# Two groups of products side by side at each phase start, and eight operand groups turned by blocks

## The chip, the cores and the metric

The kernel runs on one core of one Trainium2 chip. Its time is the device time of one execution in microseconds (us). Before the change the median of three runs is 2881.62 us (2881.26 to 2881.76).

## The reference

Two transformer blocks of width 2048 are applied in turn to 256 tokens, in float32. What costs time is the products with the weights, each of which is read once:

```python
# first block
proj = rms_norm(x) @ w_in             # q, k, v, gla q/k/v/r, decay gate, conv, 3 merge gates
mixed = g0 * (attn @ w_br_attn) + g1 * (gla @ w_br_gla) + g2 * (conv @ w_br_conv)
x = x + mixed @ w_out
h2 = rms_norm(x)
x = x + (silu(h2 @ w_ffn_gate) * (h2 @ w_ffn_up)) @ w_ffn_down
x = rms_norm(x)
# second block
proj = rms_norm(x) @ w_in_2 + b_in_2  # q, k, v, u of a scan, 2 gates
merged = sig(ga) * (attn2 @ w_branch_attn) + sig(gs) * (ssm @ w_branch_ssm)
x = x + merged @ w_out_2
val, gate = split(rms_norm(x) @ w_up)
x = x + (val * gelu(conv(gate))) @ w_down
return rms_norm(x)
```

The widths: 15376 columns in w_in, 5632 in the feed-forward, 5888 in w_in_2. Attention, gated linear attention and the scan work on 256 tokens and are small beside the weights.

## The kernel before

**Products.** A weight matrix is cut into groups of up to 512 columns (`prod` appends a Group). A group's k runs over tiles of 128 rows, 16 of them for width 2048. For the accuracy of float32 each operand is split into a high and a low part, and a product is three matmuls (lines 1395 to 1397): high by high, high by low, low by high, for each of the two halves of the tokens. A *unit* is four k-tiles, 1 MB of weights in one DMA (line 1358), with three buffers in turn; a *step* is two k-tiles, twelve matmuls. ACT writes the high part of the weights (line 165) and VectorE the low part (line 166), three steps ahead, into four buffers. The program has 1012 steps, numbered from 0.

**Operands.** The left side of a product is the activations, with the features on the partitions. So what one group of columns gives, 256 tokens by 512 features, must be transposed and split before it can be a *k-group* (four k-tiles) of the next phase. There are two ways. `to_T` uses TensorE: two halves of four 128x128 transposes each (`turn`, line 174), which ACT and VectorE split out of PSUM (lines 229, 232 with a scale, 165 and 166 without). `to_B` goes by blocks (`blocks`): VectorE transposes blocks of 32x32 (line 182), five calls later SP issues eight DMAs of 32 KB (line 187), in the next call eight more, and in the call after that the result is split (lines 209, 212 with a scale). SP issues the weights' DMAs too, all in one queue.

**Order.** The program is written out step by step in the main loop: issue the DMA of the weights five steps ahead, split three steps ahead, products, and then one call to each running job (`step_jobs`). A group that ends starts its `done` job, which reads the accumulators out. Each engine works through its own instructions in this order and waits on semaphores. The *phases* begin where the operand of the one before is complete: w_in at step 0, w_out at step 296 (operand m1), gate and up of the first feed-forward at 328 (x2), the last part of its down at 576, w_in_2 at 592 (x3), w_out_2 at 716 (m2), w_up at 748 (x4), the last part of w_down at 996. A residual's column group g gives k-group g of the next operand (`residual`); the last column group of the merge does so for m1 and m2 (`mix`).

**Where the diff touches.** `mix` turns m1's first three groups by blocks, the other five groups of m1 and m2 on TensorE; `residual` turns the first three column groups by blocks (the first two for x3) and the others on TensorE. The decay gate's group A_DN has 128 columns: its steps are six short matmuls (lines 1387 to 1389), and the flag `among` puts its units between those of the first key group. All groups else run one after the other, except in the list of units:

```python
        if g.among:
            held = own
            continue
        for u in own:
            units += [u, held.pop(0)] if held else [u]
```

Bias rows come by DMA on SP as well (`bias_tile`, three buffers in turn), ahead of the group's first weights. Four of these, fw0 to fw3, hold the final norm's weights of the first block, read by `weigh` (line 730) when a column group of the last down part ends.

Of the kernel before, what the change touches and what calls it, by code (L numbers as in the profile page):

```python
# [26 lines left out]
Q_A, K_A, V_A = 0, 1024, 2048  # L27
# [16 lines left out]
class Group:  # L44


    def __init__(self, w, nk, ncols, st, ready, done, after=None, turned=None):

        self.w, self.nk, self.ncols, self.st, self.turned = w, nk, ncols, st, turned
        self.ready, self.done, self.after = ready, done, after  # L50
        self.among = False


@with_exitstack
def two_blocks(ctx: ExitStack, tc: tile.TileContext, a: dict, out: bass.AP):
    nc = tc.nc
# [183 lines left out]
    def drop(name):  # L240
        for h, l in ACTIVE.pop(name).values():
            free(h, l)
# [17 lines left out]
    X = {}  # L260
# [411 lines left out]
    def mix(dst, key, gate, first, last, name, g):  # L672

        def done(acc):
            t = ACTIVE[gate].pop(key)
            if first:
                ACTIVE.setdefault(dst, {})[key] = t
                for tok in range(2):
                    DVE.tensor_tensor(t[:, tok, :], acc[tok], t[:, tok, :], op=ALU.mult)
                return  # L680
            m = ACTIVE[dst][key]
            for tok in range(2):
                DVE.tensor_tensor(t[:, tok, :], acc[tok], t[:, tok, :], op=ALU.mult)  # L683
            if not last:
                POOL.tensor_tensor(m, m, t, op=ALU.add)  # L685
                free(t)
                return
            DVE.tensor_tensor(m, m, t, op=ALU.add)
            free(t)
            if name == "m1" and g < 3:  # L690
                yield from to_B(lambda tok: m[:, tok, :], name, g, drop=[ACTIVE[dst].pop(key)])
                return
            yield from lag()
            yield from to_T(lambda tok: m[:, tok, :], name, g)
            free(ACTIVE[dst].pop(key))
        return done

    def residual(g, nxt=None, scale=None, parts=None, final=False, prescale=None, parts0=None):

        def done(acc):  # L700
# [20 lines left out]
            if g == 3:  # L721
                start(rms_total(nxt, parts, parts0))
            yield
            turn_it = to_B if g < (2 if nxt == "x3" else 3) else to_T
            yield from turn_it(lambda tok: X[g][:, tok, :], nxt, g, scale)
        return done

    def weigh(dst, src, name, g):
# [4 lines left out]
    groups = []  # L733
# [9 lines left out]
    def in1(c0, done, ncols=512, after=None):  # L743
        prod(w1, c0, ncols, 0, KT, "x1", done, after)

    sc1 = 1.0 / math.sqrt(128.0)
    for i in range(2):
        in1(Q_A + 512 * i, turned("qT", i, "x1", sc1))
    def ad_done(acc):
        t = galloc([16, S])  # L750
        DVE.tensor_copy(t, acc[0][0:16, 0:S])
        ACTIVE["ad"] = t
        ev.add("ad0")
        return
        yield

    in1(A_DN, ad_done, ncols=128)
    groups[-1].turned = lambda k: tuple(t[:, k % 4, :] for t in ACTIVE["x1"][k // 4])
    groups[-1].among = True
    for i in range(2):  # L760
        in1(K_A + 512 * i, turned("kT", i, "x1"))
    for i in range(2):
        in1(V_A + 512 * i, keep("v", i, "x1"))

# [41 lines left out]
    for g in range(4):  # L806
        prod(a["w_out"][0], 512 * g, 512, 0, KT, "m1", residual(g, "x2", lambda k: col("norm2", k), np2),
             after=(lambda: drop("m1")) if g == 3 else None)


    def silu_done(name, key, rs):
# [11 lines left out]
    def feed_forward(gate, up, down):  # L823


        for part, after in zip(parts, parts[1:] + [None]):
            for g in part:
                if g != part[0] or g == 0:
                    gate(g)
                up(g, part)  # L830
            if after:
                gate(after[0])
                for g in range(4 if part != parts[-2] else 3):
                    down(g, part, False)
        down(3, parts[-2], False)
        for g in range(4):
            down(g, parts[-1], True)

    def gate1(g):
        prod(a["w_ffn_gate"][0], 512 * g, 512, 0, KT, "x2", silu_done("sg", g, "x2"))  # L840
# [354 lines left out]
        ev.add("y20")  # L1195

    in2(U_2, turned2("u", 0, U_2, 1.0))
    in2(Q_2, turned2("q2", 0, Q_2, 0.125))
    in2(KV_2, kv_done, ncols=256)
    in2(Q_2 + 512, turned2("q2", 1, Q_2 + 512, 0.125))  # L1200
# [62 lines left out]
    for g in range(4):  # L1263
        prod(a["w_out_2"][0], 512 * g, 512, 0, KT, "m2", residual(g, "x4", lambda k: col("g_ffn", k), np4, prescale="x3in"),
             after=(lambda: drop("m2")) if g == 3 else None)

    def cgate_done(g):
        def done(acc):
# [59 lines left out]
    units, steps = [], []  # L1328
    held = []
    for g in groups:  # L1330
        own = [dict(g=g, k0=k0, nk=min(UK, g.nk - k0)) for k0 in range(0, g.nk, UK)]
        if g.among:
            held = own
            continue
        for u in own:
            units += [u, held.pop(0)] if held else [u]
        assert not held
    for ui, u in enumerate(units):
        for kk in range(0, u["nk"], HK):
# [2 lines left out]
    issued, split_done = [0], [0]  # L1342

    def issue(upto):
        while issued[0] < min(upto, len(units)):
            u = units[issued[0]]
            g = u["g"]
            if u["k0"] == 0 and getattr(g, "before", None):
                g.before()
            if 0 < issued[0] < 4:  # L1350
                load_xT(issued[0], nc.sync)
            elif issued[0] in (4, 5):
                load_x(2 * issued[0] - 8)
                load_x(2 * issued[0] - 7)
            u["w"] = wp.tile([128, UK, 512], F32, tag="w", name=f"w{issued[0]}")
            n = u["nk"] if issued[0] else 1
            for k in range(0, u["nk"], n):
# [49 lines left out]
    for i, s in enumerate(steps):  # L1407
# [15 lines left out]
        if s["last"]:  # L1423
            if g.after:
                g.after()
            start(g.done(g.acc))
        step_jobs()
    g = groups[-1]
    last_rows(0, g.acc[0])
    for r in steps[final:]:  # L1430
# [39 lines left out]
```

## Time and profile before

| | |
|---|---|
| median of 3 runs | 2881.62 us |
| profiled execution | 2880.97 us |
| its span, first to last instruction | 2879.3 us |
| TensorE busy | 2849.8 us (99%) |
| VectorE, ACT busy | 1759.3 us, 1314.3 us |
| HBM read | 551.51 MB, 192 GB/s over the span |
| granted TensorE clock, mean | 0.997 |

A profile is of one execution. PE is TensorE, DVE is VectorE, SPq is the DMA queue of SyncE. Matmuls overlap, so that the time of one in a row is longer than the distance to the next; the distance is what counts. A row of the timeline merges equal instructions that follow each other; what stands in brackets is how long the engine was idle before and what ended it. The clock is a share of 2.4 GHz. A row of SP's queue is the issue of DMAs, not their transfer.

### The profile page before, as it was taken

How to read it: one execution, taken by the hardware profiler on the slowest of the kernel's cores; microseconds unless marked ns; L12 is line 12 of the kernel's file. 1: busy time of each engine (PE TensorE's matmuls, PEld its weight loads, DVE VectorE, ACT ScalarE, POOL GpSimd, SP SyncE). 2: the span in 40 equal slices, each digit the busy share in tenths (PEclk: the TensorE clock that was granted, in tenths of full speed). 3: DMA queues.
4: the chain of work that ended last, by engine and by line, in shares of the span. 5: the costliest groups of instructions: out<-in, count | busy, mean ns of one | idle time of the engine just before them, and what ended most of it. 6: DMA issues, size and time to landing. Idle time of an engine off the chain costs nothing.

```text
span 2879.3 us, 33813 instructions
## 1 busy us (share of the span) xinstructions
PE 2849.8 (99%) x12819; PEld 2332.6 (81%) x12819; DVE 1759.3 (61%) x2033; ACT 1314.3 (46%) x1601; POOL 270.6 (9%) x515
## 2 busy tenths in 40 slices
PE   9999999999999999999999999999999999999998
PEld 7787787888888888888888887778888788888886
DVE  5555554555566755555555678985665666656756
ACT  5454344444444444444444454445454444434444
POOL 0000000000000590000000018600000000000000
PEclk9999999999999999999999999999999999999999
DMA  7645564655666666665665655455567677767774
GB/s 243 225 161 191 178 220 160 214 190 197 209 226 201 209 202 206 198 205 195 198 213 192 224 169 174 151 178 198 183 227 244 217 249 229 245 220 241 238 233 156
DMA packets 324570, 590.91 MB, mean 205 GB/s; under 512 B 27955, under 2 KB 53171, under 8 KB 324406
## 3 DMA queue, kind: packets, MB, share of 16 engines
q1 hardware_dynamic: 323974, 588.17, 62.3%
q8 instruction: 100, 1.64, 0.2%
q10 hardware_dynamic: 432, 0.58, 0.1%
q14 instruction: 64, 0.52, 0.1%
HBM read 551.51 MB, written 2.10 MB: 192 GB/s over the span
## 4 chain that ended last, share of the span: by engine, by line
PE 88%; DVE 4%; DMA 4%; SPq 2%; ACT 1%; issue 1%; ACTq 0%; POOLq 0%; POOL 0%; DVEq 0%
PE acc L1395 28%; PE acc L1396 28%; PE acc L1397 28%; DVE l L166 2%; SPq L187 2%; DMA w<-in_w_in_dram 1%; DMA g<-g 1%; DMA g<-in_conv_w_dram 1%; ACT h L165 1%; DMA w<-in_w_ffn_gate_dram 0%; DMA w<-in_w_up_dram 0%; PE b L174 0%; PE b L408 0%; PE b L591 0%; PE b L589 0%
## 5 line engine op out<-in xcount | busy, mean ns | idle before, releaser
L166 DVE TENSOR_TENSOR l<-w,h 128x1024 fp32r<-128x1024 f32 (+2 forms) x1013 | 1240.6, 1230 | 971.4 <-ACT h L165 957.5
L165 ACT ACTIVATE h<-w 128x1024 fp32r<-128x1024 f32 (+2 forms) x1013 | 1057.5, 1049 | 1254.1 <-PE acc L1397 1179.2
L1395 PE MATMUL acc<-h,g 128*128 128x512 f32 x4016 | 1573.1, 392 | 9.8 <-ACT h L165 5.0
L1396 PE MATMUL acc<-l,g 128*128 128x512 f32 x4016 | 1563.8, 389 | 4.3 <-DVE l L166 4.3
L1397 PE MATMUL acc<-h,g 128*128 128x512 f32 x4016 | 1562.6, 389 | 0.3 <-DVE g L318 0.3
L1395 PEld LDWEIGHTS acc<-h,g 128*128 128x128 f32 x4016 | 755.6, 188 | 175.3 <-ACT h L165 7.4
L1396 PEld LDWEIGHTS acc<-l,g 128*128 128x128 f32 x4016 | 755.7, 188 | 162.0 <-DVE l L166 8.9
L1397 PEld LDWEIGHTS acc<-h,g 128*128 128x128 f32 x4016 | 755.5, 188 | 158.8 <-DVE g L166 0.8
L252 POOL TENSOR_TENSOR s<-s,half_pow 128x2 f32<-128x2 f32 (+1 forms) x11 | 11.0, 1003 | 1322.7 <-DVE s L251 1322.7
L1119 POOL TENSOR_TENSOR g<-g,t 128x4 f32<-128x4 f32 (+7 forms) x128 | 69.5, 543 | 10.0
L621 POOL MEMSET g<- 1x512 f32 (+1 forms) x26 | 13.0, 518 | 528.7 <-DVE g L639 183.0
L1119 POOL TENSOR_TENSOR g<-g,pw_tri 128x4 f32<-128x4 f32 (+7 forms) x128 | 62.0, 484 | 0.4
L1119 POOL TENSOR_TENSOR t<-g,pw_rem 128x4 f32<-128x4 f32 (+7 forms) x128 | 61.1, 477 | 0.0
L182 DVE STREAM_TRANSPOSE g<-g 128x512 f32<-128x512 f32 x82 | 53.1, 686 | 0.1
L166 DVE TENSOR_TENSOR g<-g,g 128x512 fp32r<-128x512 f32 (+1 forms) x55 | 36.0, 696 | 25.1 <-ACT g L165 25.1
L165 ACT ACTIVATE g<-g 128x512 fp32r<-128x512 f32 (+1 forms) x55 | 32.1, 629 | 31.3 <-DMA g<-g 31.0
L703 DVE TENSOR_TENSOR g<-acc,g 128x512 f32<-128x512 f32 x70 | 44.9, 682 | 0.0
L685 POOL TENSOR_TENSOR g<-g,g 128x1024 f32<-128x1024 f32 x4 | 10.5, 2624 | 354.4 <-DVE g L683 354.4
L375 ACT ACTIVATE g<-acc,s 128x512 f32<-128x512 f32 x50 | 33.8, 689 | 20.1 <-PE acc L1397 20.1
L649 DVE SCALAR_TENSOR_TENSOR g<-acc,s,g 128x512 f32<-128x512 f32 x52 | 36.5, 744 | 0.0
L363 ACT ACTIVATE g<-acc,s 128x512 f32<-128x512 f32 x46 | 29.9, 683 | 9.8 <-PE acc L1397 7.8
L165 ACT ACTIVATE g<-b 128x512 fp32r<-128x512 f32 (+1 forms) x24 | 12.6, 526 | 47.3 <-PE b L174 21.2
(254 smaller groups left out, 889.9 us busy)
## 6 DMA issues: line engine op xcount, KB each, us to landing
w<-in_w_in_dram SPq DMA_DIRECT2D x163, 1024.0 KB
w<-in_w_up_dram SPq DMA_DIRECT2D x88, 1024.0 KB
w<-in_w_ffn_gate_dram SPq DMA_DIRECT2D x44, 1024.0 KB
w<-in_w_ffn_up_dram SPq DMA_DIRECT2D x44, 1024.0 KB
w<-in_w_ffn_down_dram SPq DMA_DIRECT2D x44, 1024.0 KB
w<-in_w_down_dram SPq DMA_DIRECT2D x44, 1024.0 KB
w<-in_w_out_dram SPq DMA_DIRECT2D x32, 1024.0 KB
g<-g SPq DMA_DIRECT2D x656, 32.0 KB
```

Source lines behind the costliest of these rows:

```text
L165: ACT.activation(h, src, AF.Copy)
L166: DVE.tensor_tensor(l, src, f32(h), op=ALU.subtract)
L182: DVE.transpose(t[:, :, tok], src(tok).rearrange("p (k g c) -> p g k c", g=4, c=32))
L187: nc.sync.dma_start(r[32 * g:32 * g + 32, i], t[32 * i:32 * i + 32, g])
L363: ACT.activation(dst[:, tok, :], acc[tok], AF.Copy, scale=rs[:, tok:tok + 1])
L375: ACT.activation(t[:, tok, :], acc[tok], func, scale=RS[rs][:, tok:tok + 1])
L649: DVE.scalar_tensor_tensor(t[:, tok, :], acc[tok], RS[rs][:, tok:tok + 1], t[:, tok, :], op0=ALU.mult, op1=ALU.mult)
L703: DVE.tensor_tensor(X[g][:, tok, :], acc[tok], X[g][:, tok, :], op=ALU.add)
L1119: POOL.tensor_tensor(o, p, q, op=op)
L1395: PE.matmul(o, lhsT=xh, rhs=h, start=(k == 0), stop=False)
L1396: PE.matmul(o, lhsT=xh, rhs=l, start=False, stop=False)
L1397: PE.matmul(o, lhsT=xl, rhs=h, start=False, stop=(k == g.nk - 1))
```

## The change

Each unit list now lets the first of two groups give way: a group with the flag `alt` is held, and its units are dealt out one by one ahead of those of the next group, so that two groups run side by side, two steps each. The flag is set on the first group of each phase named above, and in the query projection and on the first key group, whose partner is the decay gate. The first feed-forward groups are written in another order, so that the gates 0 and 1 stand next to each other. All of m1's and three of m2's groups, and all groups of x2, x3 and x4, go by `to_B`. In the decay gate's steps the jobs are called only in the last one. Loads of x and its transpose at the program's start come at other units.

```diff
@@ mix
-            if name == "m1" and g < 3:
+            if name == "m1" or g > 0:
                 yield from to_B(lambda tok: m[:, tok, :], name, g, drop=[ACTIVE[dst].pop(key)])
@@ residual
-            turn_it = to_B if g < (2 if nxt == "x3" else 3) else to_T
-            yield from turn_it(lambda tok: X[g][:, tok, :], nxt, g, scale)
+            yield from to_B(lambda tok: X[g][:, tok, :], nxt, g, scale)
@@
+    def alternate():
+
+        groups[-1].alt = True
+
     for i in range(2):
         in1(Q_A + 512 * i, turned("qT", i, "x1", sc1))
+        if i == 0:
+            alternate()
...
+    in1(K_A, turned("kT", 0, "x1"))
+    alternate()
     in1(A_DN, ad_done, ncols=128)
     groups[-1].turned = lambda k: tuple(t[:, k % 4, :] for t in ACTIVE["x1"][k // 4])
-    groups[-1].among = True
-    for i in range(2):
-        in1(K_A + 512 * i, turned("kT", i, "x1"))
+    in1(K_A + 512, turned("kT", 1, "x1"))
@@ feed_forward
             for g in part:
-                if g != part[0] or g == 0:
+                if g == 0:
+                    gate(0)
+                    alternate()
+                if g != part[0] and g != 1:
                     gate(g)
+                if g == 0:
+                    gate(1)
                 up(g, part)
...
         for g in range(4):
             down(g, parts[-1], True)
+            if g == 0:
+                alternate()
@@ (the same two lines after w_out's and w_out_2's first group; alternate() after in2(U_2, ...))
@@ units
-        if g.among:
+        if g.alt:
             held = own
             continue
         for u in own:
-            units += [u, held.pop(0)] if held else [u]
+            units += [held.pop(0), u] if held else [u]
@@ issue
-            if 0 < issued[0] < 4:
-                load_xT(issued[0], nc.sync)
-            elif issued[0] in (4, 5):
...
+            if issued[0] in (1, 3, 5):
+                load_xT((issued[0] + 1) // 2, nc.sync)
+            elif issued[0] in (6, 7):
...
@@ main loop
-        step_jobs()
+        if not g.turned or s["last"]:
+            step_jobs()
```

How this moves instructions is seen in the order in which each engine's program stands, at three places. In these rows w is a unit of weights, g an activation tile, bias a bias row; h and l with a number are the split weights of that step.

The first place is SP at the start of the second block's w_in (x3): from the bias of the scan's input group on. Before:

```order
L862 DMA bias_12130<-in_b_in_dram 128x512
L1358 DMA w_12132<-in_w_in_dram 128x4x512
L187 DMA g_311_12150<-g_306_12044 32x256 x16
L1358 DMA w_12191<-in_w_in_dram 128x4x512
L1358 DMA w_12252<-in_w_in_dram 128x4x512
L187 DMA g_318_12270<-g_309_12127 32x256 x16
L1358 DMA w_12320<-in_w_in_dram 128x4x512
L862 DMA bias_12390<-in_b_in_dram 128x512
```

The same place after the change:

```order
L1375 DMA w_12156<-in_w_in_dram 128x4x512
L876 DMA bias_12198<-in_b_in_dram 128x512
L1375 DMA w_12200<-in_w_in_dram 128x4x512
L187 DMA g_313_12218<-g_308_12110 32x256 x16
L1375 DMA w_12256<-in_w_in_dram 128x4x512
L187 DMA g_317_12288<-g_309_12151 32x256 x16
L1375 DMA w_12329<-in_w_in_dram 128x4x512
L1375 DMA w_12393<-in_w_in_dram 128x4x512
L187 DMA g_327_12411<-g_314_12253 32x256 x16
L1375 DMA w_12460<-in_w_in_dram 128x4x512
L1375 DMA w_12508<-in_w_in_dram 128x4x512
L187 DMA g_333_12526<-g_321_12381 32x256 x16
```

Four groups of sixteen blocks stand there instead of two, and the second bias row, which stood behind both groups, now stands ahead of the first.

The second place is ACT at the start of w_out_2 (m2), from the weights of step 721 to those of step 726. Before:

```order
L165 ACTIVATE h721_15628<-w360_15546 128x1024
L165 ACTIVATE g16_518_15619<-b2_521_15644 128x512
L165 ACTIVATE h722_15653<-w361_15601 128x1024
L165 ACTIVATE h723_15669<-w361_15601 128x1024
L165 ACTIVATE h724_15687<-w362_15651 128x1024
L165 ACTIVATE h725_15703<-w362_15651 128x1024
L165 ACTIVATE h726_15721<-w363_15685 128x1024
```

After:

```order
L165 ACTIVATE h721_15665<-w360_15588 128x1024
L165 ACTIVATE g26_514_15683<-g19_513_15630 128x4x4x32 x2
L165 ACTIVATE h722_15700<-w361_15639 128x1024
L165 ACTIVATE h723_15724<-w361_15639 128x1024
L165 ACTIVATE g13_517_15740<-g4_516_15689 128x4x4x32 x2
L165 ACTIVATE h724_15757<-w362_15698 128x1024
L165 ACTIVATE h725_15781<-w362_15698 128x1024
L165 ACTIVATE g21_520_15797<-g2_519_15746 128x4x4x32 x2
L165 ACTIVATE h726_15805<-w363_15755 128x1024
```

Operand splits that read blocks brought by DMA now stand between the weight splits, the last of them ahead of step 726.

The third place is SP at the decay gate, from the unit of 128 columns at step 18 on. Before:

```order
L1358 DMA w_458<-in_w_in_dram 128x4x128
L187 DMA g_24_476<-g_23_387 32x256 x16
L1358 DMA w_509<-in_w_in_dram 128x4x512
L1358 DMA w_554<-in_w_in_dram 128x4x128
L1358 DMA w_583<-in_w_in_dram 128x4x512
L1358 DMA w_611<-in_w_in_dram 128x4x128
L187 DMA g_28_629<-g_27_551 32x256 x16
L1358 DMA w_656<-in_w_in_dram 128x4x512
```

After:

```order
L1375 DMA w_591<-in_w_in_dram 128x4x128
L187 DMA g_26_609<-g_23_489 32x256 x8
L1375 DMA w_628<-in_w_in_dram 128x4x512
L187 DMA g_26_609<-g_23_489 32x256 x8
L1375 DMA w_664<-in_w_in_dram 128x4x128
L187 DMA g_28_685<-g_25_531 32x256 x8
L1375 DMA w_704<-in_w_in_dram 128x4x512
L187 DMA g_28_685<-g_25_531 32x256 x8
```

The two groups of sixteen blocks come later, each in two halves with a unit of weights between.

## Rows read from the trace of the kernel before

**Rows 1.** Busy time of each engine, from the page
```profile
PE 2849.8 (99%) x12819; PEld 2332.6 (81%) x12819; DVE 1759.3 (61%) x2033; ACT 1314.3 (46%) x1601; POOL 270.6 (9%) x515
```

**Rows 2.** Windows: busy us (instructions) of PE, PEld, DVE, ACT, POOL; clock; DMA
```profile
1200.00:1300.00 100.00, 100.00 (x443) 82.78 (x442) 53.65 (x51) 45.52 (x50) 0.00 (x0) 1.00 0.64 212
```

**Rows 3.** Timeline of PE at the x3 start: start us, us, engine, line, [idle]
```profile
1668.41 0.48 PE L1395 MATMUL acc<-h,g 128*128 128x512 f32 x1
...
1677.08 0.79 PE L1395 MATMUL acc<-h,g 128*128 128x512 f32 x1 [2.95 <-ACT g L209]
```

**Rows 4.** Windows: just behind that wait
```profile
1677.10:1679.80 2.70, 2.70 (x6) 2.13 (x7) 2.15 (x8) 2.67 (x8) 0.00 (x0) 0.50 1.00 370
```

**Rows 5.** Timeline of SP's queue, issues at the x3 start
```profile
1649.69 10.73 SPq L187 DMA_DIRECT2D g<-g  x16
...
1660.51 1.08 SPq L1358 DMA_DIRECT2D w<-in_w_in_dram  x2
...
1661.68 13.31 SPq L187 DMA_DIRECT2D g<-g  x16
...
1675.09 0.53 SPq L1358 DMA_DIRECT2D w<-in_w_in_dram  x1
```

**Rows 6.** Timeline of SP's queue, decay gate
```profile
64.05 10.02 SPq L187 DMA_DIRECT2D g<-g  x16
...
74.17 9.96 SPq L1358 DMA_DIRECT2D w<-in_w_in_dram  x5
```

**Rows 7.** Timeline of PE, one half of a turn
```profile
1664.62 0.39 PE L1397 MATMUL acc<-h,g 128*128 128x512 f32 x1
...
1664.85 0.60 PE L174 MATMUL b<-ident,g 128*128 128x128 f32 x4
...
1665.52 0.40 PE L1396 MATMUL acc<-l,g 128*128 128x512 f32 x1
```

**Rows 8.** Windows: key projection's first half and decay gate
```profile
53.60:90.50 36.90, 31.33 (x146) 25.49 (x145) 13.00 (x18) 13.71 (x21) 0.00 (x0) 0.91 0.65 209
```

**Rows 9.** Timeline of ACT, the split of the weights issued at 74.17
```profile
79.41 2.62 ACT L165 ACTIVATE h<-w 128x1024 fp32r<-128x1024 f32 x4 [3.02 <-DMA w<-in_w_in_dram]
```

**Rows 10.** Timelines of PE and ACT, last part of the second feed-forward
```profile
2829.97 0.62 PE L1395 MATMUL acc<-h,g 128*128 128x512 f32 x1 [1.81 <-ACT g L165]
...
2829.29 1.15 ACT L165 ACTIVATE g<-g 128x512 fp32r<-128x512 f32 x2 [2.75 <-DMA g<-g]
```

**Rows 11.** Timeline of DVE, product with the final norm's weights, third column group
```profile
1657.72 1.23 DVE L730 TENSOR_TENSOR g<-g,bias 128x1024 f32<-128x1024 f32 x1
```

**Rows 12.** Timeline of ACT, split of the x3 start's second operand group
```profile
1676.52 1.71 ACT L209 ACTIVATE g<-g,cols 128x256 fp32r<-128x256 f32 x4 [2.95 <-DMA g<-g]
```

**Rows 13.** Timeline of DVE, sum of m2's second column group
```profile
2045.60 1.23 DVE L688 TENSOR_TENSOR g<-g,g 128x1024 f32<-128x1024 f32 x1
```

**Rows 14.** Timeline of PE, first product of step 726
```profile
2084.36 0.39 PE L1395 MATMUL acc<-h,g 128*128 128x512 f32 x1
```

**Rows 15.** Timeline of SP's queue, x2's first two operand groups
```profile
887.46 6.78 SPq L187 DMA_DIRECT2D g<-g  x8
...
910.17 5.61 SPq L187 DMA_DIRECT2D g<-g  x8
...
923.26 0.53 SPq L1358 DMA_DIRECT2D w<-in_w_out_dram  x1
```

**Rows 16.** Timeline of ACT, x2's third operand group, next weight split
```profile
950.72 1.71 ACT L209 ACTIVATE g<-g,cols 128x256 fp32r<-128x256 f32 x4 [4.76 <-DMA g<-g]
...
953.70 1.04 ACT L165 ACTIVATE h<-w 128x1024 fp32r<-128x1024 f32 x1
```

**Rows 17.** Timeline of PE, first product of step 332
```profile
956.54 0.39 PE L1395 MATMUL acc<-h,g 128*128 128x512 f32 x1
```

**Rows 18.** Timeline of PE, weights late in the second up projection
```profile
2285.81 0.50 PE L1396 MATMUL acc<-l,g 128*128 128x512 f32 x1 [0.51 <-DVE l L166]
```

**Rows 19.** Waits of SP's queue: who for whom, us in total, times, longest
```profile
SPq L1358 <- DVE l L166: 1862.1, 398, 10.9
```

More of the change, by code (lines that the diff above doesn't have):

```diff
@@ L50, in __init__ @@
         self.ready, self.done, self.after = ready, done, after
-        self.among = False
+        self.alt = False
 @with_exitstack
@@ L837, in feed_forward @@
             down(g, parts[-1], True)
+            if g == 0:
+                alternate()
     def gate1(g):
@@ L1197, in two_blocks @@
     in2(U_2, turned2("u", 0, U_2, 1.0))
+    alternate()
     in2(Q_2, turned2("q2", 0, Q_2, 0.125))
@@ L1265, in two_blocks @@
              after=(lambda: drop("m2")) if g == 3 else None)
+        if g == 0:
+            alternate()
     def cgate_done(g):
@@ L1349, in issue @@
                 g.before()
-            if 0 < issued[0] < 4:
-                load_xT(issued[0], nc.sync)
-            elif issued[0] in (4, 5):
-                load_x(2 * issued[0] - 8)
-                load_x(2 * issued[0] - 7)
+            if issued[0] in (1, 3, 5):
+                load_xT((issued[0] + 1) // 2, nc.sync)
+            elif issued[0] in (6, 7):
+                load_x(2 * issued[0] - 12)
+                load_x(2 * issued[0] - 11)
             u["w"] = wp.tile([128, UK, 512], F32, tag="w", name=f"w{issued[0]}")
```

## The prediction

> **What bounds the kernel now.** I read the page's busy line first: TensorE is busy 2849.8 of 2879.3 us [rows 1]. So 29.5 us of gaps are left, and a change can win by taking instructions off TensorE, by closing gaps, or by shortening the stretches at half clock that follow a long gap. In a stretch with nothing but weight products 443 instructions, the first and last of them overlapping an edge, fill 100 us [rows 2]: one product starts every 0.227 us, a step of twelve takes 2.72 us. (The listed duration of about 0.39 us overlaps with the next.) Where TensorE waits, it is at the start of a phase: for an operand turned by blocks (the 2.95 us wait ended by ACT L209 [rows 3]) or for weights that came late behind the block DMAs. After that wait the granted clock of the next 2.7 us is 0.50, the 1.2 GHz level, and they hold six products where twelve would fit [rows 4]: some 1.4 us more.
>
> The engine behind both kinds of wait is SP's queue. It issues the 16 DMAs of one turned group in a row: 10.8 us to the next weight DMA in one place, 13.4 us in another, where two weight DMAs stood just ahead [rows 5]; 10.1 us with short weight DMAs about [rows 6]. While it does that, no weights are asked for. Four steps of products last 10.9 us. That is the arithmetic of this case: a group each eight steps is hidden, one each four steps just fits, one each two steps does not.
>
> **Part by part.**
>
> *Transposes taken off TensorE.* One half of a turn is four transposes. Between the product at 1664.62 and the second one after them at 1665.52 lie 0.90 us where two products alone would take 0.45 [rows 7]; two halves give 0.9 us per group. Eight groups: -7.1 us, all of it on the path, since TensorE has nothing to hide it under. The splits of these groups remain, from SBUF instead of PSUM; their ACT and VectorE work lies beside products as before (VectorE is busy 61% of the span [rows 1]).
>
> The Trainium skill ("VectorE: DVE Perf Modes", Rules for kernel authors) advises TensorE for a 128x128 transpose where a PSUM destination will do; the block path here needs VectorE and 16 DMAs in its place. By that rule the eight groups should stay, and the time would stay near 2881 or rise; the trace has both sides, 0.9 us of TensorE against 10.8 us of SP, and which of them counts depends on whether SP is free.
>
> *Decay gate.* From the first step of the key projection to the end of the gate's, 36.9 us pass [rows 8]; eight full steps (21.8) and eight gate steps of six short products (6 x 0.12 = 0.72 each, 5.8) would take 27.5. So 9.3 us are lost, because 16 blocks in one piece stand before a weight DMA: it goes out at 74.17 and its split starts at 79.41 [rows 6, 9]. After the change SP's order there is 8 blocks, weights, 8, weights, 8, weights. The first eight wait for a weight DMA that needs the buffer of the stretch's third unit, free 7.8 us into it (two steps and a split); three times eight blocks at 0.63 and the weight DMAs between put the next full weights out at 24.4 us, their split at 29.6 (5.2 later, as above), the product at 30.7. TensorE is there at 27.5: 3.2 us of wait and 1.4 of clock remain. -4.7 us; bounds 0 (same lateness) and -9.3 (all gone).
>
> *Last part of the second feed-forward.* Alternation makes the second k-group of its operand due two steps later. The wait of 1.81 us there [rows 10] and 1.4 of clock behind it go: -3.2. Nothing else is late: ACT reads the data at 2829.29, and TensorE then wants it 5.4 us after it did.
>
> *Start of the second block (x3).* The 2.95 us wait for the second group goes, with its 1.4 of clock: -4.4. But the first group (x30) now ends two steps later, and the bias of the Q projection's first group, issued six steps earlier than before, stands in SP's queue ahead of its blocks. That bias takes the buffer of a tile that VectorE still reads until 1657.72 + 1.23 = 1658.95 [rows 11]; before, the blocks had started at 1649.69. Bias and one weight DMA take 0.9: blocks from 1659.9, done 1670.7, ACT's read 1.4 later and the product 0.6 after that (both as at 1675.09, 1676.52 and 1677.08 [rows 3, 5, 12]): 1672.7. TensorE stands at the step at 1668.41 - 0.85 = 1667.6 [rows 3]: wait 5.1, clock 1.4, together +6.5. The second group is in time (1684.0 against 1685.0). The third and fourth now go by blocks too, each after two weight DMAs: at 10.8 they cost 1.0 us of waits, at 13.4 they cost 7.6 with clock. I take 4. Sum +6.1; bounds 0 (if SP ran ahead of all this) and +9.7.
>
> *Output projection of the second block (m2).* Its four operand groups end two steps apart, and three are turned by blocks now. VectorE ends the sum of the first at 2046.8 [rows 13]; 1.3 of transposes (the two of one group) make 2048.1. Three groups at 11.3 (with one weight DMA each) end at 2082.0; data 1.4 later. ACT, in order, does this split (1.05) before the weight split of step 726 (1.06): 2085.5. TensorE is at that step at 2084.36 - 2.9 = 2081.5 [rows 14]. Wait 4.0, clock 1.4: +5.4; at 10.1 a group 0.4 without clock, at 13.4 it is +11.7.
>
> *Second norm of the first block (x2).* Two block groups run in a row, ahead of the scan's parameter loads. The first starts six steps later than its 887.46, less the 0.85 of a transposed group: 903; two at 11.3 end at 925.6, against 923.26. The third group is then 2.3 us later than its 950.72; ACT's 2.98 us from there to the next weight split and 1.06 for that make 957.1, where TensorE stands at 956.54 - 1.7 = 954.9 [rows 15 to 17]: +3.6 with clock; at 10.1 a group nothing, at 13.1 (the row from 910.17 to 923.26) +7.
>
> *Smaller.* Three waits near 2285 for a late weight split (0.51 us the middle one [rows 18]) lose their cause, a whole group of 16 between two weight DMAs: -1 (0 to -1.6). Operand waits at the program's start and at the last part of the first feed-forward: -1 together. At the x4 phase two groups stand in a row as in x2, but no parameter loads follow: 0. Scans and attention shift by six steps against each other on VectorE: 0, with 3 us either way, since the work is the same. With two groups open all four accumulators are in use, and the group before must be read out within two steps (5.4 us); that is the first thing its job does: 0.
>
> Sum: -7.1 - 4.7 - 3.2 + 6.1 + 5.4 + 3.6 - 1 - 1 = -1.9. The profiled execution took 2880.97 us, 1.7 more than its span, and the median is 0.65 above it: 2881.6 - 1.9 = 2879.7, put as 2880.
>
> **Rivals.** *SP keeps up*: the blocks go at 10.1 as in the first stretch, and weights prefetched three units ahead cover the backlog. For it: SP waits 1862 us in all for weight buffers [rows 19]; against it: the three bursts above are denser than any in the trace. Then x2 and m2 cost nothing, x3 +2.1, the decay gate gives 7: -7.1 - 7 - 3.2 + 2.1 - 2 = -17, 2864. The Trainium skill ("DMA: Bandwidth & Descriptors", Issuing engines are not separate DMA queues) says that a sequencer's time to issue is usually small beside the DMA; by that rule this rival is the case. The rows here speak otherwise, 0.6 us of SP for 32 KB.
>
> *SP's backlog decides (slower)*: place, the phase starts x2, x3 and m2; price, 13.1 to 13.4 us a group there, because weight DMAs in flight slow the blocks. It decides once a group costs over 12 us. Then +7, +9.7, +11.7, the decay gate -1: -7.1 - 1 - 3.2 + 28.4 - 2 = +15, 2897.
>
> *The change does little of what it says*: block DMAs stand where transposes stood, but operands are due later by as much; no stall goes or comes but the transposes' 7.1: 2874.5.
>
> **Numbers.** The forecast with its own spread (2874 to 2886) has 0.45; SP keeps up 0.20; only the transposes 0.15; the backlog decides 0.20. A measurement of this kernel tells about 0.2%, 5.8 us, from no change. The forecast lies mostly inside that, a third case just at its edge: faster 0.36, same 0.40, slower 0.24. Range 2862 to 2896: it reaches to both outer rivals and leaves out the far half of each, under 2 in 10.
>
> **What would show it.** Transposes of line 174 fall from 104 to 40. SP's rows: a bias row that ends about 1659 ahead of 16 blocks; three groups in a row from about 2048. TensorE waits of 4 to 6 us ended by ACT L209 at the x3 start and of about 4 ended by a weight split in m2; none near 2830; one long wait less near 80. The forecast is wrong if the bias does not hold up SP, or if a group of 16 in those bursts takes under 10 or over 13 us.

## The result, and the profile after

The changed kernel takes 2910.49 us (median of four runs, 2910.03 to 2911.51) against 2881.69: ratio 1.0099, 95% interval 1.0086 to 1.0112. It is slower by 1%, above the range of the prediction, which had it about 2 us faster. Its profiled execution has a span of 2908.3 us, 29.0 more than before.

TensorE is busy as long as before, within 2 us, though 64 transposes are gone (line 174 now has 40) [rows 1]:

```profile
PE 2851.8 (98%) x12755; PEld 2330.5 (80%) x12755; DVE 1767.7 (61%) x2065; ACT 1314.3 (45%) x1601; POOL 276.3 (9%) x515
```

Where the 29 us come on is read from the start of the first product of the same step in both traces. The forecast's column puts 0.9 us of saved transposes to each group turned by blocks; its small terms at the program's start and in the first feed-forward (-1) are left out. The other columns are experiments, told below (rounded one by one): e1 only the blocks, e2 only the alternation, e4 the change with GpSimd issuing the blocks, e9 the kernel before with GpSimd issuing most of them.

| stage (steps) | forecast | after | e1 | e2 | e4 | e9 |
|---|---|---|---|---|---|---|
| start and decay gate (0-296) | -4.7 | -0.4 | +0.8 | -2.2 | -10.1 | -8.6 |
| m1 (296-312) | -0.9 | -1.0 | +4.2 | 0.0 | -1.0 | 0.0 |
| x2 (312-360) | +2.7 | +4.8 | +12.7 | +6.1 | +6.9 | -1.0 |
| first feed-forward (360-576) | 0 | 0.0 | 0.0 | 0.0 | +19.0 | 0.0 |
| x3 (576-616) | +4.3 | +8.6 | +15.0 | +1.4 | +1.9 | -3.8 |
| attention, scan (616-716) | 0 | +2.8 | -0.1 | +4.2 | +4.6 | +1.3 |
| m2 (716-732) | +2.7 | +8.7 | +15.6 | 0.0 | +4.4 | 0.0 |
| x4 (732-764) | -0.9 | +6.2 | +8.3 | +4.8 | -1.0 | 0.0 |
| second up projection (764-820) | -1 | -0.1 | -2.8 | +1.5 | +1.6 | -2.8 |
| last part (820-end) | -3.2 | -0.8 | -2.0 | -2.4 | -2.0 | -2.4 |
| sum | -1.0 | +29.0 | +51.8 | +13.4 | +24.4 | -17.2 |

At the x3 start the trace of after shows what was foreseen, and more. SP's queue (start us, us, issues) [rows 5]:

```profile
1663.15 0.34 SPq L876 DMA_DIRECT2D bias<-in_b_in_dram  x1
...
1664.02 13.37 SPq L187 DMA_DIRECT2D g<-g  x16
...
1678.12 10.27 SPq L187 DMA_DIRECT2D g<-g  x16
...
1690.13 13.39 SPq L187 DMA_DIRECT2D g<-g  x16
...
1704.75 13.04 SPq L187 DMA_DIRECT2D g<-g  x16
```

and VectorE, the first operand's transposes and the product that frees the bias buffer [rows 11]:

```profile
1652.02 1.30 DVE L182 STREAM_TRANSPOSE g<-g 128x512 f32<-128x512 f32 x2
...
1661.90 1.23 DVE L729 TENSOR_TENSOR g<-g,bias 128x1024 f32<-128x1024 f32 x1
```

The first operand's blocks are ready at 1653.3, and SP stands at the bias until VectorE is done with that buffer at 1663.1. Then four groups follow each other, and three of them take over 13 us. Not all of that is issuing: sixteen blocks at 0.63 us each are 10.1, and the view of SP's waits, from 1664 to 1718, has its block DMAs wait for weight DMAs to land, 9.8 us in six times, the longest 3.1:

```profile
SPq L187 <- DMA w<-in_w_in_dram: 9.8, 6, 3.1
```

In SP's queue at m2 and x4 three groups follow each other, and two and two; ahead of m2's stand three weight DMAs that wait for buffers, and at x4 the parameter rows of two gate groups (line 615) stand in one place, and the eight blocks behind them take 9.69 us:

```profile
2050.34 15.59 SPq L1375 DMA_DIRECT2D w<-in_w_out_dram  x3
2066.02 5.80 SPq L187 DMA_DIRECT2D g<-g  x8
2072.20 0.37 SPq L1375 DMA_DIRECT2D w<-in_w_out_dram  x1
2072.62 10.79 SPq L187 DMA_DIRECT2D g<-g  x16
2083.50 0.53 SPq L1375 DMA_DIRECT2D w<-in_w_out_dram  x1
2084.07 10.67 SPq L187 DMA_DIRECT2D g<-g  x16
2094.84 0.53 SPq L1375 DMA_DIRECT2D w<-in_w_out_dram  x1
2095.42 5.71 SPq L187 DMA_DIRECT2D g<-g  x8
...
2151.73 1.69 SPq L615 DMA_DIRECT2D g<-in_conv_w_dram  x3
...
2154.47 2.23 SPq L615 DMA_DIRECT2D g<-in_conv_w_dram  x3
...
2160.58 9.69 SPq L187 DMA_DIRECT2D g<-g  x8
```

TensorE waits there (the bracket: idle us, and what ended it) [rows 3, 10, 14]. A wait for weights that stands nowhere in before is at 2251.36, in the second up projection. In the last part the long wait for an operand is gone, but three small ones for late weights stand at the very end, the first of them shown:

```profile
86.31 0.71 PE L1412 MATMUL acc<-h,g 128*128 128x512 f32 x1 [4.68 <-ACT h L165]
...
1679.47 0.79 PE L1412 MATMUL acc<-h,g 128*128 128x512 f32 x1 [8.85 <-ACT g L209]
...
1719.61 0.50 PE L1412 MATMUL acc<-h,g 128*128 128x512 f32 x1 [2.43 <-ACT g L209]
...
2093.51 0.50 PE L1412 MATMUL acc<-h,g 128*128 128x512 f32 x1 [1.07 <-ACT h L165]
...
2104.71 0.79 PE L1412 MATMUL acc<-h,g 128*128 128x512 f32 x1 [4.41 <-ACT h L165]
...
2182.14 0.76 PE L1412 MATMUL acc<-h,g 128*128 128x512 f32 x1 [2.46 <-ACT h L165]
...
2251.36 0.50 PE L1413 MATMUL acc<-l,g 128*128 128x512 f32 x1 [2.48 <-DVE l L166]
...
2886.40 0.50 PE L1413 MATMUL acc<-l,g 128*128 128x512 f32 x1 [0.76 <-DVE l L166]
```

Two windows of after: the decay gate holds 149 TensorE instructions where it held 146 [rows 8], so its loss is nearly whole (the weights that the wait at 86.31 is for stand below them, SP and then ACT); and behind m2's wait the granted clock is 0.50, as it was behind the wait of before [rows 4]:

```profile
53.60:90.50 36.90, 30.92 (x149) 25.49 (x149) 13.53 (x19) 13.09 (x20) 0.00 (x0) 0.94 0.52 160
2104.70:2110.40 5.70, 5.23 (x12) 3.76 (x12) 4.71 (x4) 2.90 (x3) 0.00 (x0) 0.50 1.05 377
```

```profile
78.46 1.52 SPq L1375 DMA_DIRECT2D w<-in_w_in_dram  x1
```

```profile
85.20 1.06 ACT L165 ACTIVATE h<-w 128x1024 fp32r<-128x1024 f32 x1 [8.51 <-DMA w<-in_w_in_dram]
```

### The profile page after: what moved, and what is told of

It is laid out like the page before. It is cut to its first block, busy times and chain, and to the rows that moved or that the text cites. A ratio compares the mean times of both kernels' runs of the same rounds, so it can differ in the third digit from the quotient of the medians.

```text
span 2908.3 us, 33936 instructions
## 1 busy us (share of the span) xinstructions
PE 2851.8 (98%) x12755; PEld 2330.5 (80%) x12755; DVE 1767.7 (61%) x2065; ACT 1314.3 (45%) x1601; POOL 276.3 (9%) x515
## 4 chain that ended last, share of the span: by engine, by line
PE 84%; DVE 5%; DMA 5%; ACT 2%; SPq 2%; issue 1%; POOL 0%; ACTq 0%; POOLq 0%; DVEq 0%
PE acc L1413 27%; PE acc L1412 27%; PE acc L1414 27%; DVE l L166 2%; SPq L187 2%; DMA w<-in_w_out_dram 1%; DMA w<-in_w_in_dram 1%; ACT h L165 1%; DMA g<-g 1%; DMA w<-in_w_down_dram 1%; DMA w<-in_w_up_dram 1%; DMA w<-in_w_ffn_gate_dram 1%; ACT junk L266 0%; DVE g L1172 0%; DVE g L182 0%
## 5 line engine op out<-in xcount | busy, mean ns | idle before, releaser
L1412 PE MATMUL acc<-h,g 128*128 128x512 f32 x4016 | 1574.4, 392 | 29.1 <-ACT h L165 17.2
L182 DVE STREAM_TRANSPOSE g<-g 128x512 f32<-128x512 f32 x98 | 63.6, 687 | 0.2
L212 DVE SCALAR_TENSOR_TENSOR g<-g,cols,g 128x128 fp32r<-128x128 f32 x112 | 30.7, 348 | 34.1 <-ACT g L209 34.1
L209 ACT ACTIVATE g<-g,cols 128x256 fp32r<-128x256 f32 x56 | 23.9, 498 | 55.2 <-DMA g<-g 55.2
L375 ACT ACTIVATE g<-acc,s 128x512 f32<-128x512 f32 x50 | 33.6, 689 | 19.6 <-PE acc L1414 19.5
```

The lines of the kernel that those rows point to most:

```text
L182: DVE.transpose(t[:, :, tok], src(tok).rearrange("p (k g c) -> p g k c", g=4, c=32))
L212: DVE.scalar_tensor_tensor(l[:, k, s], x[:, tok], scale(4 * g + k), f32(h[:, k, s]), op0=ALU.mult, op1=ALU.subtract)
L375: ACT.activation(t[:, tok, :], acc[tok], func, scale=RS[rs][:, tok:tok + 1])
L1412: PE.matmul(o, lhsT=xh, rhs=h, start=(k == 0), stop=False)
```

## The experiments

Two theories were set against each other first: A, SP's queue at the phase starts has no time for what either edit asks of it; B, the blocks are cheap and the alternation alone does the harm.

**e1, the blocks alone.** In the kernel before:

```diff
-            if name == "m1" and g < 3:
+            if name == "m1" or g > 0:
...
-            turn_it = to_B if g < (2 if nxt == "x3" else 3) else to_T
-            yield from turn_it(lambda tok: X[g][:, tok, :], nxt, g, scale)
+            yield from to_B(lambda tok: X[g][:, tok, :], nxt, g, scale)
```

> The kernel before with one edit: the eight operand groups go by blocks instead of by TensorE; no groups alternate, the decay gate is as it was. Theory A (SP's queue at the phase starts is the cost, and each of the two edits needs SP at a place where it has no time): without alternation the fourth operand group of x2 and of x4 is due six steps (16.3 us) after its column group ends; five calls of lag, 10.8 us of issues and 3 us of arrival and split do not fit, so TensorE waits some 5 us there and loses 1.4 us of clock, twice; x3's third and fourth group the same; m1 and m2 about 3 us each. About +32 against -7.1 of transposes: 2900 to 2912. Theory B (the blocks are cheap, the alternation packs them and is alone the cause): 2874 to 2885.

Measured: 2931.25 us, ratio 1.017 (1.0155 to 1.0185). The direction was A's, the size well over it. One wait in each of x2, x3 and x4 is of 7.5 to 10.4 us:

```profile
978.01 0.79 PE L1394 MATMUL acc<-h,g 128*128 128x512 f32 x1 [10.38 <-ACT g L209]
...
1710.38 0.80 PE L1394 MATMUL acc<-h,g 128*128 128x512 f32 x1 [9.38 <-ACT g L209]
...
2216.50 0.79 PE L1394 MATMUL acc<-h,g 128*128 128x512 f32 x1 [7.54 <-ACT g L209]
```

**e2, the alternation alone.** The same two places, in the changed kernel, the other way round.

> The changed kernel with the eight operand groups back on TensorE; alternation and decay gate as in the change. Theory A: m2's three bursts are gone (their 10 us of waits with them, and 2.7 us of transposes come back), x3's third and fourth group cost no waits (about -5, +1.8 of transposes); x2 and x4 keep theirs, since two block groups still end side by side there: 2910 - 10 + 2.7 - 5 + 1.8 + 2.7 = about 2902, 2896 to 2906. Theory B: all of the loss stays and the transposes come on top: 2915 to 2920.

Measured: 2893.99 us, ratio 1.0042 (1.0027 to 1.0056): less than A's range, and B is out. Neither edit is a gain alone. The blocks cost 51.8 us alone and 15.6 on top of the alternation (29.0 - 13.4); the alternation costs 13.4 alone and saves 22.8 where the blocks are there. The stage m2 is as before without its three bursts (0.0).

**e3, the bias late.** In the changed kernel, for the first two groups of the second block:

```diff
-            if u["k0"] == 0 and getattr(g, "before", None):
+            if u["k0"] == getattr(g, "bias_at", 0) and getattr(g, "before", None):
...
     alternate()
+    groups[-1].bias_at = 12
     in2(Q_2, turned2("q2", 0, Q_2, 0.125))
+    groups[-1].bias_at = 12
```

> The changed kernel; the bias rows of the second block's first two groups are fetched with the last unit of each group instead of the first, so that no bias DMA stands ahead of the first operand's blocks. In the trace of the change SP stood at that bias from 1652.7 to 1663.2 while VectorE had the blocks ready at 1653.3. Theory A: the blocks go at about 1653.7, the wait of 8.8 us and its half clock go, and what follows moves with it: 2898 to 2902. Rival: the blocks then meet the weight DMAs in flight or the next stall moves up: no more than 3 us, 2907 or more.

Measured: 2909.35 us, ratio 1.0092 (1.0077 to 1.0108): the rival's number. The wait at the first operand does go, steps 576 to 592 take as long as before, but of the 6.6 us by which this kernel is ahead of after at step 592, 1.2 are left at step 748. SP and then TensorE:

```profile
1660.07 10.88 SPq L187 DMA_DIRECT2D g<-g  x16
...
1671.67 11.31 SPq L187 DMA_DIRECT2D g<-g  x16
...
1684.25 13.35 SPq L187 DMA_DIRECT2D g<-g  x16
...
1699.30 13.99 SPq L187 DMA_DIRECT2D g<-g  x16
```

```profile
1715.20 0.50 PE L1414 MATMUL acc<-h,g 128*128 128x512 f32 x1 [3.82 <-ACT g L209]
```

The first group is issued 4 us earlier than in after (A had it 10 us earlier; SP now waits for weight buffers there), the fourth ends at 1713.3 instead of 1717.8, and the wait has moved to it. The bias was the first link of a chain whose length is SP's work.

**e4, the blocks on GpSimd.** In the changed kernel:

```diff
-                nc.sync.dma_start(r[32 * g:32 * g + 32, i], t[32 * i:32 * i + 32, g])
+                POOL.dma_start(r[32 * g:32 * g + 32, i], t[32 * i:32 * i + 32, g])
```

> The changed kernel; all block DMAs are issued by GpSimd instead of SP, so SP has only the weights and the small loads. Theory A (SP's issue time is what delays weights and blocks): the waits for weight splits near 86, 933, 959, 2094, 2105, 2182 and 2885 go, and the blocks no longer stand behind weight or bias DMAs; 29 us of loss turn into the gain of the transposes and the closed gaps: 2862 to 2875. Rival C: GpSimd needs over 1 us for an issue of 32 KB, so that a group takes over 16 us and operands come later than now: 2900 or more. Rival D: SP was not it, the DMA engines are: waits stay where they are, 2905 to 2915.

Measured: 2904.03 us, ratio 1.0078 (1.0063 to 1.0093): none of the three. Rival D's waits did not stay where they were: by stages A holds at the decay gate (9.7 us better than after), x3, m2 and x4; x2 is worse, and 19 us are lost in the first feed-forward, where nothing was lost before. There a table of small operations is in GpSimd's queue, and blocks wait behind them: those that VectorE had ready at 1086.1 are issued behind the last of the operations, at 1106.35 (GpSimd, then TensorE):

```profile
1105.67 0.73 POOL L1133 TENSOR_TENSOR g<-g,t 128x256 f32<-128x256 f32 x1
1106.35 7.88 POOL L187 DMA_DIRECT2D g<-g  x16
```

```profile
1117.63 0.80 PE L1412 MATMUL acc<-h,g 128*128 128x512 f32 x1 [6.51 <-ACT h L165]
```

Rival C is out: sixteen issues take 7.88 us, less than on SP.

**e5, m2 on TensorE.** In the changed kernel:

```diff
-            if name == "m1" or g > 0:
+            if name == "m1":
```

> The changed kernel with m2's second to fourth operand groups back on TensorE (six half turns, +2.7 us of transposes); all else as in the change. In the change TensorE lost about 10.2 us at steps 723 to 726, with three bursts of sixteen DMAs in SP's queue. Theory A (the bursts are the cause): the waits go, 2910 - 10 + 2.7 = 2902 or 2903, if x4's start keeps its own loss. Rival: m2's column groups end too late for TensorE too (alternation alone), so waits for turned groups take their place: 2910 or more.

Measured: 2901.78 us, ratio 1.0061 (1.0044 to 1.0078), as A says; steps 716 to 732 are as before to 0.0 us.

**e6, parameter rows late.** In the changed kernel, with the condition of e3:

```diff
         groups[-1].before = lambda: conv_rows(("c2", g), a["conv_w_2"][0, :, c], a["conv_b_2"][0:1, c])
+        groups[-1].bias_at = 12 if g == 1 else 0
```

> The changed kernel; in the second feed-forward the four parameter rows of the second gate group are fetched with that group's last unit instead of its first, so only four of eight small loads stand in SP's queue at the x4 start. Theory A (the eight loads, 6 us of SP between 2151.7 and 2158, are what makes x4's weights late; the prediction said that none are there): the loss of 5.4 us at steps 748 to 756 falls by 3 to 5.4, 2905 to 2907. Rival E (as the late bias showed, SP is simply full and the next burst takes the time back): within 2 us, 2908 to 2911.

Measured: 2908.41 us, ratio 1.0086 (1.0071 to 1.0101), 2 us under after and within its spread: rival E's number. The trace shows E's mechanism too. At the phase start A is right, steps 748 to 756 lose 1.4 us instead of 5.4, and the wait of 2.46 is one of 0.99. But of these 4 us all but 0.9 are lost again by step 780.

**e7, e2 with e3's late bias.**

> Alternation with the eight groups on TensorE (2894), and the bias rows of x3's first two groups late. With all of the change the late bias moved the wait of 8.8 us at the x3 start five groups of weights further, since the third and fourth group's blocks followed without a gap. Theory A (SP is full only while four block groups follow each other): with two block groups at x3 the 6 us wait there goes and does not come back: 2887 to 2889. Rival: it comes back later here too: 2892 to 2895.

Measured: 2886.52 us, ratio 1.0012 (1.0003 to 1.0021), half a us better than A's range. The stage x3 goes from +1.4 to -6.2 and the gain stays: the same edit that was worth 1 us with four block groups is worth 7 with two.

**e8, the gate's steps advance jobs.** In the changed kernel:

```diff
-        if not g.turned or s["last"]:
-            step_jobs()
+        step_jobs()
```

> The changed kernel with the decay gate's steps advancing the jobs as before the change. Theory A (what the blocks cost there is SP's time, and the flag only shifts them by some steps): the stretch from the key projection's first step to the gate's end keeps its loss within 2 us, 2908 to 2913. Rival G (the flag spreads the blocks as the prediction took it): without it the gate stage loses 4 us more, 2914. Rival H (the flag itself is what ate the gain there): 2905 or 2906.

Measured: 2916.95 us, ratio 1.0118 (1.0103 to 1.0133), 6 us over after: rival G in its sign. The groups stand in one piece again (SP, then TensorE), and a wait of 5.3 follows:

```profile
54.90 10.58 SPq L187 DMA_DIRECT2D g<-g  x16
...
66.15 10.01 SPq L187 DMA_DIRECT2D g<-g  x16
```

```profile
78.53 0.58 PE L1404 MATMUL acc<-g,h 128*128 128x256 f32 x1 [5.30 <-ACT h L165]
```

Of these 6 us the first 40 steps account for 2.1 against after, and for 2.7 to 3.9 against the other five kernels on SP's queue with after's order there (e2, e3, e5 to e7); G gives the flag 4. Most of the rest comes on between steps 600 and 660, where this edit changes nothing: stages with the same order differ by 1 to 3 us from one kernel's profile to another's, and a stage's difference of that size is not read as an effect.

**e9, the kernel before with GpSimd.** Its order unchanged; `blocks` is handed the operand's name for it, and those calls are left out here:

```diff
-            nc.sync.dma_start(r[32 * g:32 * g + 32, i], t[32 * i:32 * i + 32, g])
+            (nc.sync if name[:2] in ("x2", "h1") else POOL).dma_start(r[32 * g:32 * g + 32, i], t[32 * i:32 * i + 32, g])
```

> The kernel before, unchanged in its order, with the block DMAs issued by GpSimd, except those of x2 and of the first feed-forward, which stay on SP (there GpSimd has its table of small operations in the queue, which held blocks back for over 20 us when all went that way). Theory A (SP's issue time is the cost): the decay gate's loss of 9.3 us goes but for 1 or 2, the x3 wait of 2.95 and the last part's 1.81 with their half clock go in part, the three small waits near 2285 go: 2882 - 8 - 4 - 3 - 1 = about 2866, 2863 to 2870. Rival: the waits at x3 and in the last part are latency from the column group's end and not SP's queue: only the decay gate gains, 2872 to 2875.

Measured: 2863.72 us, ratio 0.9935 (0.9923 to 0.9947), A's number. It is faster than both kernels. The decay gate's window holds 187 TensorE instructions at full clock instead of 146 [rows 8], and the steps 16 to 33 take 33.0 us instead of 42.4; GpSimd issues the blocks there in four runs of eight, two of them shown, and the wait of 2.95 at x3 [rows 3] is gone (windows, GpSimd, TensorE):

```profile
53.60:90.50 36.90, 36.90 (x187) 31.47 (x186) 20.54 (x26) 18.69 (x26) 12.72 (x26) 1.00 0.68 218
```

```profile
57.64 3.91 POOL L187 DMA_DIRECT2D g<-g  x8 [6.86 <-DVE g L182]
61.90 3.92 POOL L187 DMA_DIRECT2D g<-g  x8 [0.34 <-DMA g<-g]
```

```profile
1665.52 0.50 PE L1397 MATMUL acc<-h,g 128*128 128x512 f32 x1 [0.73 <-DVE g L212]
```

**e10, e7 with e6's rows and e9's queues.**

> Alternation, the eight groups on TensorE, late bias and late parameter rows, and the block DMAs on GpSimd except those of x2 and of the first feed-forward. Theory A: 2886.5 with late bias, less 8 for the decay gate, less 4 at the x4 start and near 2250, less 1 at the end: 2873 or 2874, 2870 to 2877. Rival: GpSimd's DMAs wait for their own queue's room, so that only the decay gate gains: 2878 to 2880.

Measured: 2872.81 us, ratio 0.9966 (0.9954 to 0.9978), as A says, and 9 us over e9: with SP relieved the alternation still isn't a gain. By stages it loses against e9 in x2, whose blocks stay on SP (4.4 us), in attention and scan (4.4) and in the second up projection (2.8), and gains at x3 (2.9).

**e11, the whole change with all three edits.**

> The whole change (eight groups by blocks too) with late bias, late parameter rows and the block DMAs on GpSimd except those of x2 and of the first feed-forward. Theory A (the blocks are worth their transposes as soon as SP is free of them): 7 us of TensorE less than the alternating kernel with the eight groups on TensorE, so it would lie 4 to 7 us under that: 2866 to 2872. Rival: bursts of three and four groups pile up on any one queue, m2 and x3 wait again: 2878 to 2888, slower than the one with TensorE.

Measured: 2880.40 us, ratio 0.9994 (0.9986 to 1.0003): the rival, 7.6 us over e10 in spite of 7 us fewer transposes. Waits at x3 and m2 are back though SP is free of those blocks:

```profile
1686.86 0.79 PE L1415 MATMUL acc<-h,g 128*128 128x512 f32 x1 [3.22 <-ACT g L209]
...
2076.47 0.50 PE L1415 MATMUL acc<-h,g 128*128 128x512 f32 x1 [2.01 <-ACT h L165]
```

At x3 the trace shows what holds them. VectorE has the third group's blocks ready at 1660.0, but in GpSimd's queue an operation of the norm stands ahead of them and waits for VectorE, and the blocks go out at 1675.38 (VectorE, GpSimd). No run moves that operation; what holds m2's blocks was not tested.

```profile
1658.72 1.30 DVE L182 STREAM_TRANSPOSE g<-g 128x512 f32<-128x512 f32 x2
```

```profile
1673.79 1.63 POOL L252 TENSOR_TENSOR s<-s,half_pow 128x2 f32<-128x2 f32 x1 [8.73 <-DVE s L251]
1675.38 3.97 POOL L187 DMA_DIRECT2D g<-g  x8
```

**e12, e10 without the alternation at x3** (its `alternate()` and the late bias taken out).

> The alternating kernel with GpSimd (2873) without the alternation of the second block's first two groups and without the late bias rows; the other phases still alternate. In every kernel that alternates there, 4 to 5 us come on between steps 616 and 716 (attention and scan), whatever queue carries the blocks; in the two that don't, none. Theory A (alternating those two groups shifts their jobs against attention and scan on TensorE's way): that stretch falls to within 1.5 us of before, and the time to about 2868, 2866 to 2870. Rival: the stretch depends on the earlier phases' order, and keeps its 5 us: 2872 or more.

Measured: 2874.42 us, ratio 0.9972 (0.9961 to 0.9983), the rival's number. The stretch did as A said, +1.3 instead of +5.7 in steps 616 to 716; the time didn't, since steps 576 to 616 take 3.7 us more without the alternation. (x2 and the steps near 775, which both kernels have alike, differ by another 3.0 us.) At x3 the alternation pays at the phase start and gives it back in attention and scan, where TensorE waits longer for ACT's results. The wait at one such place is 2.66 us in e10 and 0.53 in e12; here it is in before and in after:

```profile
1835.75 0.43 PE L932 MATMUL b<-g,g 128*64 128x128 f32 x2 [0.70 <-ACT g L450]
```

```profile
1849.01 0.43 PE L946 MATMUL b<-g,g 128*64 128x128 f32 x2 [2.65 <-ACT g L450]
```

## Why the prediction was wrong, step by step

The engine named was right: SP's queue. The forecast and the trace lie 30 us apart. Of these x4 gives 7.1, m2 6.0, the decay gate and x3 4.3 each, attention and scan 2.8, the last part 2.4, x2 2.1. The step that failed is the price of SP's work at the phase starts: SP was taken to be free when a burst's blocks are ready, a group was priced by the lower of two rows, and x4's parameter rows were put at nothing. Beside it failed the price of the clock behind a wait and some terms that were put at nothing for alternating.

The rival that was given 0.20, that SP's backlog decides, came nearer. Without the transposes x2 measured +5.7 (that rival 7, forecast 3.6), x3 +10.4 (9.7 and 6.1), m2 +10.3 in steps 720 to 728 (11.7 and 5.4). How near is luck in part: in m2 its price of 13.4 us a group was not met, and at x3 the first group met it too, which had 10.8 in that rival's sum as in the forecast's.

- *x3.* The bias row, the buffer and the waiting blocks are as described; the trace stands 3.5 us later by then, and so the blocks start at 1664.0 less 3.5, 1660.5 where 1659.9 was worked out. The group was put at 10.8 and took 13.4 [rows 5], with one weight DMA just ahead of it and not two, and TensorE waited 8.85 instead of 5.1. A group over 13 us was the forecast's own sign of being wrong; it came three times. e3 and e7 show that the size of the loss is that of the whole chain of four groups, not of the bias.
- *m2.* VectorE's sum ended when foreseen (2063.1, in a trace that is 16.3 us later by then). The blocks, ready at 2064.4, were taken to start at once; SP was at weight DMAs that waited for buffers and started them at 2066.0. The three groups took 11.7 each with their weights and not 11.3, still not the 12 at which that rival was to decide. The weights of step 724 came late as well, so TensorE waited at two steps, not one, and the first product of step 726 came 7.0 late instead of 4.0. What stood behind that wait took another 3.3 instead of 1.4. e5 shows the stage whole.
- *Clock.* 1.4 was put behind each wait, from one row [rows 4]. Behind m2's wait 12 products took 5.70 us (the second window above) where 2.7 are full speed: 3.0 more, of which about 1.0 is not the clock but the second product's wait for the low part of the same weights (it starts 1.26 after the first). The trace of before has that price too, behind its wait near 80, 13 products in 6.00 us (the row below). Worked out in the same way at the four waits that had the term (decay gate, x2, x3, m2), it is some 6 of the 30 us. At x2 it is the larger part of the miss: the wait itself came as forecast, 2.32 us at 958.57 against 2.2.

```profile
80.50:86.50 6.00, 5.52 (x13) 4.04 (x14) 3.02 (x4) 1.52 (x3) 0.00 (x0) 0.55 0.70 229
```

- *x4* was put at 0, "no parameter loads follow". That was a misreading: the gate groups of the second feed-forward fetch parameter rows by the same hook as bias tiles, and with two gate groups side by side eight loads stand together. The stage is SP's, since with the blocks on GpSimd nothing is lost there (e4, -1.0). How loads and blocks share it is not shown: e6 takes half of the loads away and loses nearly all of that again some steps later.
- *Decay gate*, -4.7, came out near the upper bound given, 0: the stage gave -0.4, and -1.0 to -2.2 in the five kernels with the same order there (e2, e3, e5 to e7). The full weights went out at 78.46, 1.3 after the time worked out (52.8 + 24.4 = 77.2), and took 6.7 to their split instead of 5.2; the product is at 86.31 instead of 83.5. The split into halves did not suffice. e9's 187 instructions, and its 33.0 us instead of 42.4, show that the whole 9.3 us were SP's.
- *Attention and scan*, 0 "since the work is the same", gave +2.8, and +4.2 up to step 712, where the first of m2's transposes are saved. Up to there every kernel that alternates at x3 loses 4.1 to 7.1 us, and e1, e9 and e12, which do not, at most 1.3: the alternation at x3 makes it. Equal work on VectorE and ACT does not mean equal waits on TensorE, whose attention products stand between weight products in a fixed order.
- *Second up projection*, -1: the three waits near 2285 went (-2.8 in steps 780 to 820), but they went in e1 too, whose order there is that of before, so that this is not the change's gain. The wait of 2.48 at 2251.36 took it back; every kernel that alternates has it (+2.8 to +4.4), e10 as well, so SP's blocks are not its cause. VectorE works there without a break from 2228 to 2254, with the products and sums of the gate groups (lines 635 to 643) between the weight splits.
- *Last part*, -3.2 and measured -0.8: the wait near 2830 went as foreseen, with its half clock (-3.6 by step 1008), and 2.9 us came on in the last four steps, where weights are late. Why they are late there was not tested; e9 gains 2.4 there.
- *Transposes*, -7.1: they left TensorE, and what took their place cost more than they gave back on either queue, 15.6 us on SP's (after against e2) and 7.6 on GpSimd's (e11 against e10).

The Trainium skill's rule ("VectorE: DVE Perf Modes", Rules for kernel authors), TensorE for a 128x128 transpose where PSUM will do, was the better guide here; e1, e5 and e11 agree with it. The same skill's remark that a sequencer's time to issue is usually small beside the DMA ("DMA: Bandwidth & Descriptors", Issuing engines are not separate DMA queues) does not hold in this kernel: SP takes 0.63 us or more for each 32 KB, and e9 moves nothing but who issues 27 groups, and gains 17.2 us of span. How much of that is issuing, and how much SP's waiting for weight DMAs to land between the blocks, no run separates.

## What to carry to other kernels

Where one queue issues both prefetches and many small transfers, count its issue time per phase like an engine's busy time, with everything that is in the queue by the same hook, and put no term at the lower of two rows when the new burst is denser than either. Price what follows a wait from all such stretches in the trace, not from one. A wait that is taken from the head of such a chain moves to its end; what helps is work taken off the queue. Move the small transfers to a sequencer that is idle in that stretch, and look in its trace for long runs of its own operations, and for operations that wait, first (e4 against e9, e11).

## What was not expected of the hardware

GpSimd issues these 32 KB DMAs in 0.49 us each (3.91 for eight), SP in 0.63 to 0.75 where it is quick, and in 0.84 on the mean of the sixteen that go out at 1664.02 of after (13.37 us), since it stops in between until a weight DMA has landed. The two edits are far from additive: 51.8 and 13.4 us apart, 29.0 together. The whole change without most of SP's share (e11) stands where the kernel before stood.
